# A two-layer hybrid trunk: DeltaNet's triangular inversion in 32x32 blocks, and gate and up weights in rows and places of 16 KB

## The chip, the cores and the metric

One core of a Trainium2 chip. The metric is the device time of one execution in microseconds, the median of three runs. The engines are TensorE (PE for its matmuls, PEld for its weight loads), VectorE (DVE), ScalarE (ACT), GpSimd (POOL) and SyncE (SP), which here issues every transfer from HBM.

## The reference, cut to what matters

Two layers, each a token mixer and then a mixture of experts, both closed by a layer norm. 256 tokens of width 1024, everything in float32. For the change two places matter:

```python
# gated DeltaNet, one of three mixers: 4 chunks of 64 tokens x 4 heads = 16 systems of 64x64
amat = beta[..., :, None] * jnp.einsum('bhcid,bhcjd->bhcij', k, k) * decay   # strictly lower
lhs = amat + jnp.eye(CHUNK, dtype=f32)
sol = lax.linalg.triangular_solve(lhs, rhs, left_side=True, lower=True, unit_diagonal=True)
...
# experts: 32 of them, weights 1024x512, 1024x512 and 512x1024 each, all read in every layer
for e in range(N_EXPERTS):
    h = jax.nn.silu(xt @ w_gate[e]) * (xt @ w_up[e])
    y = y + combine[:, e:e + 1] * (h @ w_down[e])
```

The expert weights of a layer are 192 MiB, those of the mixer about 50 MiB.

## The kernel before

Each layer has two stages. In the **mixer** stage the main line of work is a list of 26 blocks (`ORDER`): projections of x, branch projections and the output projection. A block's weights come in four slabs of 512 KB; each slab is split by ACT and DVE into a high and a low half (`split`, lines 252 and 264), and TensorE multiplies three times (`mm3`). The mixers' own chains (`delta_chain`, `ret_chain`, `ssd_chain`) are generators; `Weave` runs one step of each after every piece of the main line, so their matmuls stand between those of the projections. The order on each engine is fixed when the kernel is built, by the framework's scheduler, which estimates when each instruction can start; each engine, and SP's list of transfers, then runs in that order.

`delta_chain` inverts its sixteen unit lower triangular matrices by doubling. Two matrices (the two heads of a pair) stand one above the other in 128 partitions, eight such pairs side by side: a tile of 128x512. `at` is the transpose of `am` (one matmul by the identity for each block, tile `pat`). `Tn` and `Tt` hold the inverse of the diagonal blocks of size s and its transpose. In round s = 2, 4, 8, 16, 32 a mask on POOL (`mask`) cuts the blocks below the diagonal out of `at`; `px` = bt, Tn; `xx` is its copy; `pn` and `pT` are the corrections of `Tn` and `Tt` (`pn` not in the last round). Each of these products, `bmm`, is 16 matmuls of 64x64x64, on two 64x64 tiles of the array in turn: the upper pair's on rows and columns 0 to 63, the lower pair's on 64 to 127. The trace shows each float32 matmul as two weight loads and two matmul records.

In the **expert** stage eight sets of four experts follow each other. `set_front` gathers each expert's tokens with a one-hot matrix (tile `pxg`), `set_mlp` multiplies by the gate (`pg`) and up (`pu`) weights, `set_tail` by the down weights (`pdn`), `set_scatter` adds to the tokens (`acc`). The four experts of a set take 32 columns of the array each. A set's weights are 24 transfers of 1 MiB, each of 128 rows of 8 KB (`rows`, `W`): gate in two halves of four experts, up in two halves, down in two halves. Which token feature stands in which partition follows from that layout (`ROW`). The last set's down weights come in smaller pieces.

The weights live in **places** of 8 KB per partition. `ring` hands them out in a cycle: `wp` has 9; `wb` adds 6 when the mixers' working pool `mx` (20 tiles) closes after block mA; `wd` adds 2 after block mC1; `wc` adds 7 at the end of the mixer stage, 24 in all. `AT` says where in the cycle the new ones are put. A transfer waits until every reader of the place's former content is done; a mixer block takes two places, and the gain and bias of a layer norm (`W_ln`) one place each. Eight semaphores are used for the transfers, in turn, so at most eight are under way.

Of the kernel before, what the change touches and what calls it, by code (L numbers as in the profile page):

```python
# [10 lines left out]
F32 = mybir.dt.float32  # L11
# [25 lines left out]
EQ = 4  # L37
# [22 lines left out]
def _constants():  # L60

    f = np.float32
    p = np.arange(128)
    i64 = np.arange(64)
    par, loc = p // 64, p % 64
    c = {}
    c["ident"] = np.eye(128)
    c["alpha"] = np.eye(128) * ALPHA
    c["ut"] = (par[:, None] == par[None]) & (p[:, None] <= p[None])
    c["bo"] = par[:, None] == par[None]  # L70
    c["he"] = (par == 0)[:, None]
# [3 lines left out]
    for s in (1, 2, 4, 8, 16, 32):  # L75

        c[f"mt{s}"] = ((loc[:, None] // (2 * s) == i64[None] // (2 * s))
                       & (loc[:, None] % (2 * s) < s) & (i64[None] % (2 * s) >= s))
    c["m1"] = ((loc[:, None] // 2 == i64[None] // 2) & (loc[:, None] % 2 == 1) & (i64[None] % 2 == 0))
# [82 lines left out]
def trunk_kernel(ctx: ExitStack, tc: tile.TileContext, x_in, w_in, w_br, w_g, w_u, w_d, smalls, lnp, consts, out,  # L162
# [37 lines left out]


    places = ["wp"] * WP

    def ring(name="w"):
        cnt[0] += 1
        k = places.pop(0)
        places.append(k)
        return (wp if k == "wp" else pools[k][1]).tile([128, 2048], F32, name=f"{name}{cnt[0]}", tag="w")

    def more_places(name, n, side, at):  # L210
        open_pool(name, n, side)
# [3 lines left out]
        close_pool(name)  # L215
        places[:] = [k for k in places if k != name]

    def rows(src, u):

        return src[u:u + 2].rearrange("u p f -> (u p f)").rearrange("(q f) -> q f", f=2048)  # L220

    def ROW(k):

        u, j, kk = k // 4, k // 2 % 2, k % 2
        return lambda a: [a.rearrange("p (u h k q j) -> p u h k q j", h=2, k=2, q=64, j=2)[:, u, h, kk, :, j] for h in range(2)]

    def W(src):
        w = ring()
        nc.sync.dma_start(w, src)
        return w  # L230

# [171 lines left out]
    for l in range(layers):  # L403
# [254 lines left out]
        def delta_chain():  # L658
# [66 lines left out]
            pt = P("pat")  # L725
# [6 lines left out]
            DVE.tensor_copy(at, pt)  # L732
            Tn, Tt = T("Tn"), T("Tt")
            mb = lambda k: C[k][:, None, :].to_broadcast([128, 8, 64])
            POOL.tensor_mul(o8(Tn), o8(am), mb("m1"))
            POOL.tensor_sub(o8(Tn), C["e64b"], o8(Tn))
            DVE.tensor_mul(o8(Tt), o8(at), mb("mt1"))
            DVE.tensor_sub(o8(Tt), C["e64b"], o8(Tt))

            def mask(s):  # L740
                b = T("bt", True)
                POOL.tensor_mul(o8(b), o8(at), mb(f"mt{s}"))
                return b

            bt = mask(2)
# [7 lines left out]
                vb.append(vt)  # L753
            R["av"] = None
            yield
            blocks = [(n, par) for n in range(8) for par in range(2)]

            def bmm(p, a, b):
                for n, par in blocks:
                    ps, cs = slice(64 * par, 64 * par + 64), slice(n * 64, n * 64 + 64)  # L760
                    mm(p[ps, cs], a[ps, cs], b[ps, cs])

            for s in (2, 4, 8, 16, 32):
                px = P("px")
                bmm(px, bt, Tn)
                yield
                xx = T("xx", True)
                DVE.tensor_copy(xx, px)
                if s < 32:
                    bt = mask(2 * s)  # L770
                yield
                if s < 32:
                    pn = P("pn")
# [7 lines left out]
                if s < 32:  # L781
                    yield
            v4 = lambda t: t.rearrange("p (h d) -> p h d", h=4)
            yield
            for tt in range(NT):
# [527 lines left out]


        def set_front(i):
            e = EQ * i
            oh = T("oh")
            ohv = oh.rearrange("p (u t e s) -> p u t e s", u=2, t=2, e=EQ)
            it = C["iota"][:, None, None, 0:PL].to_broadcast([128, 2, EQ, PL])
            DVE.tensor_tensor(ohv[:, 0], it, bc(pv[:, :, e:e + EQ, None], PL), op=OP.is_equal)  # L1320
            POOL.tensor_mul(ohv[:, 1], ohv[:, 0], bc(cv[:, :, e:e + EQ, None], PL))  # L1321

            def gather(k0, n, copy, pin=False):

                p, t = P("pxg"), T("xg")
                for k in range(n):
                    for tt in range(NT):
                        for hh, xc in enumerate(ROW(k0 + k)(x[:, tt])):
                            m = mm(p[64 * hh:64 * hh + 64, k * 128:(k + 1) * 128], xc,
                                   oh[:, tt * 128:(tt + 1) * 128], tt == 0, tt == 1)  # L1330
# [12 lines left out]

            return gather, back

        def set_mlp(i, xg, more=None):
            e = EQ * i
            pg, pu = P("pg"), P("pu")
            for p, src in ((pg, w_g), (pu, w_u)):
                for k in range(KD):  # L1350
                    if k == len(xg):
                        xg += more(k)
                    if k % 4 == 0:
                        ws = [W(rows(src[l, e + a], k // 2)).rearrange("p (k f) -> p k f", k=4) for a in range(EQ)]
# [12 lines left out]
            return hr  # L1367
# [41 lines left out]
        def overflow(mxi):  # L1409
# [5 lines left out]
            with tc.If(rv > thresh):  # L1415
                with tc.For_i(0, NE, 1) as ei:

                    room = [wp.tile([128, 2048], F32, name=f"wo{cnt[0]}_{j}", tag="w") for j in range(WP)]
# [145 lines left out]
```

## Time and profile before

| | us |
|---|---|
| median of three runs | 1631.17 (1630.39 to 1631.46) |
| profiled execution, its own time | 1631.13 |
| its span, first to last instruction | 1629.5 |

Of the span TensorE is busy 84%, its weight loads 54%, VectorE 39%, ScalarE 31%, GpSimd 12%. The shares hide two different stages, each run through twice: mixers with a busy TensorE and a DMA that is a third busy, and experts with a DMA that is full. The page therefore has to be read in the stretches of its second part (40 slices of 40.7 us), not in its totals.

### The profile page before, as it was taken

What the parts mean: (1) busy time and instruction counts of PE and PEld (TensorE: products, weight loads), DVE (VectorE), ACT (ScalarE), POOL (GpSimd) and SP (SyncE); (2) the same over time, 40 slices, a digit from 0 to 9 for tenths busy, and PEclk for the clock granted to TensorE, in tenths of its full rate; (3) what the DMA queues carried; (4) which work ended last, traced back from release to release, by engine and by line L of the source; (5) the groups of instructions that cost most, each with busy time, mean ns of one, the idle gap of its engine ahead of it and who ended that gap; (6) DMA issues with size and microseconds to landing.
All of it is one profiled execution on the core that took longest, in us unless ns stands there. A gap on an engine that the chain in (4) does not pass through costs nothing.

```text
span 1629.5 us, 25989 instructions
## 1 busy us (share of the span) xinstructions
PE 1371.3 (84%) x10670; PEld 877.0 (54%) x10670; DVE 634.8 (39%) x1194; ACT 504.1 (31%) x997; POOL 188.2 (12%) x158
## 2 busy tenths in 40 slices
PE   8999999999877728866799999999998677287775
PEld 8999878985312203211289998799843122132211
DVE  6887777763000000000188887776620000000002
ACT  5846657541000000000067565685310000000000
POOL 0230243200000000000014212422000000000000
PEclk9999999999989959989899999999999999699889
DMA  9543333879999999999984443348799999999996
GB/s 382 182 155 130 129 131 105 317 292 411 427 427 426 427 426 426 426 427 426 409 318 132 144 141 104 134 141 346 293 408 427 428 425 426 427 427 426 427 427 257
DMA packets 90411, 518.96 MB, mean 318 GB/s; under 512 B 10032, under 2 KB 10672, under 8 KB 42928
## 3 DMA queue, kind: packets, MB, share of 16 engines
q1 hardware_dynamic: 90288, 517.25, 78.9%
q8 instruction: 86, 1.41, 0.3%
q14 instruction: 37, 0.30, 0.1%
HBM read 516.16 MB, written 1.05 MB: 317 GB/s over the span
## 4 chain that ended last, share of the span: by engine, by line
DMA 49%; PE 46%; DVE 3%; issue 1%; ACT 1%; SPq 0%; DVEq 0%
DMA w<-in_w_u_dram 19%; DMA w<-in_w_g_dram 14%; DMA w<-in_w_d_dram 14%; PE g L261 9%; PE pbr L261 6%; PE cx L261 3%; PE cz L261 3%; PE pout L261 3%; PE aq L261 1%; PE cbc L261 1%; PE av L261 1%; PE bq L261 1%; PE ak L261 1%; PE az L261 1%; PE bg L261 1%; PE pdn L261 1%
## 5 line engine op out<-in xcount | busy, mean ns | idle before, releaser
L252 DVE TENSOR_TENSOR hi<-w,hi 128x512 fp32r<-128x512 f32 x400 | 324.5, 828 | 84.2 <-ACT hi L264 37.4
L1366 DVE TENSOR_TENSOR hr<-h,pu 128x256 f32<-128x256 f32 x32 | 16.7, 599 | 726.7 <-PE pu L261 726.7
L264 ACT ACTIVATE hi<-w 128x512 fp32r<-128x512 f32 x400 | 242.8, 629 | 144.1 <-PE pbr L261 35.8
L261 PE MATMUL pg<-w,xg 128*32 128x512 f32 x1024 | 190.4, 667 | 114.4 <-DMA w<-in_w_g_dram 114.2
L261 PE MATMUL pu<-w,xg 128*32 128x512 f32 x1024 | 194.1, 673 | 61.1 <-DMA w<-in_w_u_dram 61.1
L261 PEld LDWEIGHTS pg<-w,xg 128*32 128x32 f32 x1024 | 43.7, 119 | 245.7 <-issue 138.2
L261 PE MATMUL pdn<-w,ht 128*32 128x512 f32 x1024 | 145.6, 614 | 26.5 <-DMA w<-in_w_d_dram 13.7
L261 PEld LDWEIGHTS pu<-w,xg 128*32 128x32 f32 x1024 | 45.6, 120 | 190.1 <-DMA w<-in_w_u_dram 110.0
L261 PE MATMUL g<-xh,hi 128*128 128x256 f32 x768 | 143.4, 285 | 0.0
L261 PEld LDWEIGHTS g<-xh,hi 128*128 128x128 f32 x768 | 120.7, 191 | 6.2 <-issue 5.8
L264 ACT ACTIVATE h<-pg 128x512 f32<-128x512 f32 x16 | 9.6, 597 | 338.7 <-PE pg L261 338.7
L261 PE MATMUL g<-xl,hi 128*128 128x256 f32 x384 | 108.9, 284 | 0.0
L261 PEld LDWEIGHTS pdn<-w,ht 128*32 128x32 f32 x1024 | 36.4, 112 | 121.8 <-issue 71.7
L1321 POOL TENSOR_TENSOR oh<-oh,cmb 128x256 f32<-128x256 f32 x16 | 10.0, 623 | 760.2 <-DVE oh L1320 654.9
L261 PE MATMUL pbr<-yh,hi 128*128 128x256 f32 x512 | 95.4, 283 | 0.0
L264 ACT ACTIVATE xg<-pxg 128x512 f32<-128x512 f32 (+1 forms) x18 | 10.3, 574 | 247.5 <-PE pxg L261 247.5
L264 ACT ACTIVATE os<-pdn 128x512 f32<-128x512 f32 x32 | 19.1, 596 | 215.7 <-PE pdn L261 140.9
L261 PEld LDWEIGHTS pbr<-yh,hi 128*128 128x128 f32 x512 | 80.4, 190 | 0.8 <-issue 0.3
L261 PE MATMUL pxg<-oh,x 128*64 128x128 f32 x1024 | 59.9, 274 | 21.9 <-DVE oh L1320 18.3
L261 PEld LDWEIGHTS pxg<-oh,x 128*64 128x64 f32 x1024 | 56.0, 138 | 34.9 <-issue 26.2
L261 PEld LDWEIGHTS g<-xl,hi 128*128 128x128 f32 x384 | 73.5, 191 | 0.1
L261 PE MATMUL pbr<-yl,hi 128*128 128x256 f32 x256 | 73.0, 285 | 0.0
(351 smaller groups left out, 2209.2 us busy)
## 6 DMA issues: line engine op xcount, KB each, us to landing
w<-in_w_g_dram SPq DMA_DIRECT2D x128, 1024.0 KB, 19.5
w<-in_w_u_dram SPq DMA_DIRECT2D x128, 1024.0 KB, 19.6
w<-in_w_d_dram SPq DMA_DIRECT2D x112, 1024.0 KB, 19.6
w<-in_w_in_dram SPq DMA_DIRECT2D x152, 512.0 KB, 4.7
w<-in_w_br_dram SPq DMA_DIRECT2D x48, 512.0 KB, 4.7
w<-in_w_d_dram SPq DMA_DIRECT2D x24, 512.0 KB, 11.8
ln<-in_lnp_dram SPq DMA_DIRECT2D x8, 512.0 KB, 10.7
w<-in_w_d_dram SPq DMA_DIRECT2D x16, 256.0 KB, 7.5
```

What stands on the lines that cost most here:

```text
L252: return DVE.tensor_sub(l, src, lo(h))
L261: return PE.matmul(o, l, r, start=start, stop=stop)
L264: return ACT.activation(o, i, f, **k)
L1321: POOL.tensor_mul(ohv[:, 1], ohv[:, 0], bc(cv[:, :, e:e + EQ, None], PL))
L1366: DVE.tensor_mul(hr.rearrange("p (j k h q) -> p h k q j", j=2, k=2, h=2)[:, hh], v(h), v(pu))
```

## The change

The inversion works in blocks of 32x32. The sixteen 64x64 matrices have 32 diagonal blocks; each of the four groups of 32 partitions holds eight of them side by side, 128x256 in all, and `bmm` is 32 matmuls of 32x32x32, on the four diagonal 32x32 tiles of the array in turn. The rounds are s = 2, 4, 8, 16. `Tn` and `Tt` are the halves of one tile, and both corrections come into one PSUM tile and are taken off by one DVE instruction. The block below the diagonal is done at the end: its transpose is fetched early (`pao`, 16 matmuls from partition groups 1 and 3 to 0 and 2), and two products of 16 matmuls each and their copies then fill the full 64x64 inverse (`Tf`).

The second part gives the places 16 KB: `unit` hands out a whole one, `ring` a half. `wp`, `wb`, `wd`, `wc` have 4, 3, 1 and 4 (in halves 8, 6, 2 and 8, where there were 9, 6, 2 and 7), and `mx` has 24 tiles. In all sets but the first, gate and up weights come as one transfer of 2 MiB for each expert, 128 rows of 16 KB, and `set_front` gathers in four column groups of 32 where there were two of 64. Down weights keep rows of 8 KB.

```diff
-WP, WB, WC = 9, 6, 7
-SP, MX, MS, MB, WD = 8, 20, 6, 4, 2
-AT = 4, 6, 7
+WP, WB, WC = 4, 3, 4
+SP, MX, MS, MB, WD = 8, 24, 6, 4, 1
+AT = 2, 3, 4
...
+    halves = []
+    def unit(name="w"):
+        assert not halves
         cnt[0] += 1
         k = places.pop(0)
         places.append(k)
-        return (wp if k == "wp" else pools[k][1]).tile([128, 2048], F32, name=f"{name}{cnt[0]}", tag="w")
+        return (wp if k == "wp" else pools[k][1]).tile([128, 4096], F32, name=f"{name}{cnt[0]}", tag="w")
+    def ring(name="w"):
+        if not halves:
+            w = unit(name)
+            halves.extend((w[:, 0:2048], w[:, 2048:4096]))
+        return halves.pop(0)
...
+            quarter = [slice(32 * q, 32 * q + 32) for q in range(4)]
...
+            def bmm(p, a, b):
+                for n in range(8):
+                    for q in quarter:
+                        mm(p[q, d32(n)], a[q, d32(n)], b[q, d32(n)])
+            pt, pf = P("pat"), P("pao")
             for n in range(8):
-                for par in range(2):
-                    ps = slice(64 * par, 64 * par + 64)
-                    mm(pt[ps, n * 64:n * 64 + 64], am[ps, n * 64:n * 64 + 64], ident[ps, ps])
+                for i, q in enumerate(quarter):
+                    mm(pt[q, d32(n)], am[q, c32(n, i % 2)], ident[q, q])
+            for n in range(8):
+                for e in range(2):
+                    mm(pf[quarter[2 * e], d32(n)], am[quarter[2 * e + 1], c32(n)],
+                       ident[quarter[2 * e + 1], quarter[2 * e + 1]])
...
+            for i, q in enumerate(quarter):
+                POOL.tensor_mul(o32(Tn)[q], o8(am)[q, :, 32 * (i % 2):32 * (i % 2) + 32], mb("m1")[q])
...
-            for s in (2, 4, 8, 16, 32):
+            for s in (2, 4, 8, 16):
                 px = P("px")
                 bmm(px, bt, Tn)
                 yield
-                xx = T("xx", True)
-                DVE.tensor_copy(xx, px)
-                if s < 32:
+                xx = T("xx", True)[:, :256]
+                DVE.tensor_copy(xx, px[:, :256])
+                if s < 16:
                     bt = mask(2 * s)
                 yield
-                if s < 32:
-                    pn = P("pn")
-                    bmm(pn, Tt, xx)
-                pT = P("pT")
-                bmm(pT, xx, Tt)
+                pn = P("pn")
+                bmm(pn, Tt, xx)
+                bmm(pn[:, 256:], xx, Tt)
                 yield
-                if s < 32:
-                    DVE.tensor_sub(Tn, Tn, pn)
-                DVE.tensor_sub(Tt, Tt, pT)
+                DVE.tensor_sub(TT, TT, pn)
+                yield
+            px = P("px")
+            for n in range(8):
+                for e in range(2):
+                    mm(px[quarter[2 * e + 1], d32(n)], at[quarter[2 * e], 256 + n * 32:288 + n * 32], Tn[quarter[2 * e], d32(n)])
...
+            pT = P("pT")
+            for n in range(8):
+                for e in range(2):
+                    mm(pT[quarter[2 * e], d32(n)], xx[quarter[2 * e + 1], d32(n)], Tt[quarter[2 * e + 1], d32(n)])
+            yield
+            for e in range(2):
+                act(o8(Tf)[quarter[2 * e], :, 32:64], o32(pT[quarter[2 * e], :256]), AF.Copy, scale=-1.0)
...
-                    if k % 4 == 0:
+                    if i == 0 and k % 4 == 0:
                         ws = [W(rows(src[l, e + a], k // 2)).rearrange("p (k f) -> p k f", k=4) for a in range(EQ)]
+                    elif k == 0:
+                        ws = [W2(rows(src[l, e + a], 0, 4)).rearrange("p (k f) -> p k f", k=8) for a in range(EQ)]
                     for a in range(EQ):
                         ps = slice(PL * a, PL * a + PL)
-                        mm(p[ps], xg[k][:, ps], ws[a][:, k % 4], k == 0, k == KD - 1)
+                        mm(p[ps], xg[k][:, ps], ws[a][:, k % (4 if i == 0 else 8)], k == 0, k == KD - 1)
```

## Rows read from the trace of the kernel before

**Rows 1.** The page's second part: busy tenths of 40 slices, and GB/s.

```profile
PE   8999999999877728866799999999998677287775
DMA  9543333879999999999984443348799999999996
GB/s 382 182 155 130 129 131 105 317 292 411 427 427 426 427 426 426 426 427 426 409 318 132 144 141 104 134 141 346 293 408 427 428 425 426 427 427 426 427 427 257
```

**Rows 2.** Stretches: length, busy us of five engines (instructions), granted clock, DMA share, GB/s.

```profile
20.00:30.00 10.00, 10.00 (x86) 10.00 (x85) 9.64 (x27) 7.69 (x14) 0.00 (x0) 1.00 1.02 419
...
100.00:160.00 60.00, 60.00 (x743) 56.29 (x743) 47.23 (x104) 35.32 (x59) 5.03 (x6) 1.00 0.42 139
...
342.50:362.50 20.00, 20.00 (x91) 16.50 (x90) 13.86 (x22) 6.29 (x12) 1.29 (x1) 1.00 0.59 193
362.50:385.00 22.50, 20.86 (x145) 13.10 (x145) 13.74 (x56) 2.88 (x8) 0.67 (x1) 1.00 1.00 414
385.00:387.50 2.50, 2.50 (x40) 1.89 (x44) 0.00 (x0) 0.60 (x1) 0.00 (x0) 1.00 0.73 218
387.50:700.00 312.50, 228.81 (x1626) 79.44 (x1618) 16.32 (x32) 17.64 (x32) 3.70 (x6) 0.90 1.01 426
```

**Rows 3.** The chain that ended last, 88 to 172 us: start, us, what.

```profile
88.57 1.15 PE pat L261 x32
...
96.21 1.08 PE px L261 x32
97.29 3.30 PE cx L261 x26
100.59 1.08 PE pn L261 x32
101.67 0.93 PE pT L261 x32
...
167.04 0.49 PE pT L261 x12
...
167.97 0.73 PE pT L261 x20
```

**Rows 4.** Instructions in order of time: four column tiles of 32, 512 columns each.

```profile
516.41 3.63 PE L261 MATMUL pg<-w,xg 128*32 128x512 f32 x28 [1.03 <-DMA w<-in_w_g_dram]
```

**Rows 5.** SP's transfers around the end of the first mixer stage.

```profile
331.45 0.80 SPq L229 DMA_DIRECT2D w<-in_w_g_dram  x2
334.99 19.19 SPq L229 DMA_DIRECT2D w<-in_w_d_dram  x5
360.60 0.33 SPq L229 DMA_DIRECT2D w<-in_w_g_dram  x1
363.51 2.98 SPq L229 DMA_DIRECT2D w<-in_w_u_dram  x6
368.12 2.29 SPq L229 DMA_DIRECT2D w<-in_w_d_dram  x2
...
384.95 5.80 SPq L229 DMA_DIRECT2D w<-in_w_g_dram  x5
```

**Rows 6.** What SP waited for from 280 to 420 us: total, times, longest.

```profile
SPq L229 <- DVE hi L252: 43.6, 10, 6.5
SPq L229 <- PE pg L261: 12.4, 2, 11.4
```

**Rows 7.** Instructions in order of time: the last set's tail, first and second layer.

```profile
786.23 6.52 PE L261 MATMUL pu<-w,xg 128*32 128x512 f32 x26 [1.40 <-DMA w<-in_w_u_dram]
...
1593.65 3.62 PE L261 MATMUL pu<-w,xg 128*32 128x512 f32 x26 [1.46 <-DMA w<-in_w_u_dram]
...
1599.97 3.41 PE L261 MATMUL pdn<-w,ht 128*32 128x512 f32 x22 [0.78 <-DVE ht L1385]
...
1611.88 3.63 PE L261 MATMUL pdn<-w,ht 128*32 128x512 f32 x28 [2.24 <-DMA w<-in_w_d_dram]
```

**Rows 8.** The page's third part: a DMA queue's packets, MB, share of 16 engines.

```profile
q8 instruction: 86, 1.41, 0.3%
```

More of the change, by code (lines that the diff above doesn't have):

```diff
@@ L74, in _constants @@
     c["madd"] = np.where(i64[None] < loc[:, None], 0.0, -30000.0)
[L75 to L79, printed above, removed]
+    i32, l32 = np.arange(32), p % 32
+    for s in (1, 2, 4, 8, 16):
+        c[f"mt{s}"] = ((l32[:, None] // (2 * s) == i32[None] // (2 * s))
+                       & (l32[:, None] % (2 * s) < s) & (i32[None] % (2 * s) >= s))
+    c["m1"] = (l32[:, None] // 2 == i32[None] // 2) & (l32[:, None] % 2 == 1) & (i32[None] % 2 == 0)
+    c["d32"] = l32[:, None] == i32[None]
     inv = (f(10000.0) ** (-np.arange(0, 128, 2, dtype=f) / f(128))).astype(f)
@@ L216, in fewer_places, with rows, ROW, W2 @@
         places[:] = [k for k in places if k != name]
[L218 to L225, printed above, removed]
+    def rows(src, u, n=2):
+        return src[u:u + n].rearrange("u p f -> (u p f)").rearrange("(q f) -> q f", f=1024 * n)
+    def ROW(k, n):
+        u, j, kk = k // (2 * n), k // 2 % n, k % 2
+        return lambda a: [a.rearrange("p (u h k q j) -> p u h k q j", h=n, k=2, q=128 // n, j=n)[:, u, h, kk, :, j]
+                          for h in range(n)]
     def W(src):
         w = ring()
+        nc.sync.dma_start(w, src)
+        return w
+    def W2(src):
+        w = unit()
         nc.sync.dma_start(w, src)
@@ L724, in delta_chain @@
             yield
-            pt = P("pat")
-            for n in range(8):
-                for par in range(2):
-                    ps = slice(64 * par, 64 * par + 64)
-                    mm(pt[ps, n * 64:n * 64 + 64], am[ps, n * 64:n * 64 + 64], ident[ps, ps])
+            quarter = [slice(32 * q, 32 * q + 32) for q in range(4)]
+            c32 = lambda n, r=0: slice(n * 64 + 32 * r, n * 64 + 32 * r + 32)
+            d32 = lambda n: slice(n * 32, n * 32 + 32)
+            o32 = lambda a: a.rearrange("p (n j) -> p n j", j=32)
@@ L730, in delta_chain @@
             yield
             at = T("at")
[L732 to L738, printed above, removed]
+            DVE.tensor_copy(at[:, :256], pt[:, :256])
+            for e, eng in ((0, DVE.tensor_copy), (1, act)):
+                eng(at[quarter[2 * e], 256:], pf[quarter[2 * e], :256])
@@ L740, in mask @@
+            TT = T("Tn")
+            Tn, Tt = TT[:, :256], TT[:, 256:]
+            mb = lambda k: C[k][:, None, :].to_broadcast([128, 8, 32])
+            for i, q in enumerate(quarter):
+                POOL.tensor_mul(o32(Tn)[q], o8(am)[q, :, 32 * (i % 2):32 * (i % 2) + 32], mb("m1")[q])
+            POOL.tensor_sub(o32(Tn), mb("d32"), o32(Tn))
+            DVE.tensor_mul(o32(Tt), o32(at[:, :256]), mb("mt1"))
+            DVE.tensor_sub(o32(Tt), mb("d32"), o32(Tt))
             def mask(s):
-                b = T("bt", True)
@@ L742, in mask @@
-                POOL.tensor_mul(o8(b), o8(at), mb(f"mt{s}"))
+                b = T("bt", True)[:, :256]
+                POOL.tensor_mul(o32(b), o32(at[:, :256]), mb(f"mt{s}"))
                 return b
@@ L755, in delta_chain @@
             yield
[L756 to L761, printed above, removed]
-            for s in (2, 4, 8, 16, 32):
+            for s in (2, 4, 8, 16):
                 px = P("px")
@@ L766, in delta_chain @@
                 yield
-                xx = T("xx", True)
-                DVE.tensor_copy(xx, px)
-                if s < 32:
+                xx = T("xx", True)[:, :256]
+                DVE.tensor_copy(xx, px[:, :256])
+                if s < 16:
                     bt = mask(2 * s)
                 yield
-                if s < 32:
-                    pn = P("pn")
-                    bmm(pn, Tt, xx)
-                pT = P("pT")
-                bmm(pT, xx, Tt)
-                yield
-                if s < 32:
-                    DVE.tensor_sub(Tn, Tn, pn)
-                DVE.tensor_sub(Tt, Tt, pT)
-                if s < 32:
-                    yield
+                pn = P("pn")
+                bmm(pn, Tt, xx)
+                bmm(pn[:, 256:], xx, Tt)
+                yield
+                DVE.tensor_sub(TT, TT, pn)
[4 more added lines that the diff above has]
+                    mm(px[quarter[2 * e + 1], d32(n)], at[quarter[2 * e], 256 + n * 32:288 + n * 32], Tn[quarter[2 * e], d32(n)])
+            Tf = T("Tt")
+            POOL.tensor_copy(o8(Tf)[:, :, 0:32], C["zero"][:, :, None].to_broadcast([128, 8, 32]))
+            for i, q in enumerate(quarter):
+                (POOL.tensor_copy if i < 2 else act)(o8(Tf)[q, :, 32 * (i % 2):32 * (i % 2) + 32], o32(Tt)[q])
+            yield
+            xx = T("xx", True)
+            for e, eng in ((0, DVE.tensor_copy), (1, act)):
+                eng(xx[quarter[2 * e + 1], :256], px[quarter[2 * e + 1], :256])
+            yield
+            pT = P("pT")
+            for n in range(8):
+                for e in range(2):
+                    mm(pT[quarter[2 * e], d32(n)], xx[quarter[2 * e + 1], d32(n)], Tt[quarter[2 * e + 1], d32(n)])
+            yield
+            for e in range(2):
+                act(o8(Tf)[quarter[2 * e], :, 32:64], o32(pT[quarter[2 * e], :256]), AF.Copy, scale=-1.0)
+            Tt = Tf
             v4 = lambda t: t.rearrange("p (h d) -> p h d", h=4)
@@ L1315, in set_front @@
         def set_front(i):
-            e = EQ * i
+            e, nr = EQ * i, 2 if i == 0 else 4
             oh = T("oh")
@@ L1416, in overflow @@
                 with tc.For_i(0, NE, 1) as ei:
-                    room = [wp.tile([128, 2048], F32, name=f"wo{cnt[0]}_{j}", tag="w") for j in range(WP)]
+                    room = [wp.tile([128, 4096], F32, name=f"wo{cnt[0]}_{j}", tag="w") for j in range(WP)]
+                    room = [r[:, c:c + 2048] for r in room for c in (0, 2048)]
                     ws = []
```

5 lines of the change are left out of this document (2 added, 3 removed).

## The prediction

> **What bounds the kernel now.** I read the slices first [rows 1]: four stages, two with PE at 9 tenths and DMA at 3 to 5 (mixers), two with DMA at 9 (experts). The stretches [rows 2] say how hard each limit is. From 100 to 160 us PE is busy 60.00 of 60.00 us at full clock while DVE has 47 and DMA 0.42 of its time: the mixer is TensorE's. From 387.5 to 700 us DMA has a share of 1.01 and 426 GB/s while PE has 229 of 312 us: the expert stage is the DMA's, and PE's clock (0.90) matters there only at its end. The chain [rows 3] confirms the first: it runs through PE alone, and the inversion's products stand on it one after the other between projections. Between the stages lies a third stretch that belongs to neither: from 342.5 to 362.5 us DMA has only 0.59 [rows 2], because SP waits for places, 43.6 us on weights not yet split [rows 6]. From 362.5 on DMA is full but for one hole, 385 to 387.5 us (0.73), where SP waits for set 0's gate to free a place [rows 5, 6]. So whatever still has to be loaded when the last places open, at 360.6 us [rows 5], shifts the end one to one. That is the view that decides here.
>
> **Part 1, the inversion on PE.** Before, for each layer: pat 1.15 us, five px at 1.08, four pn at 1.08, four pT at 0.93 and the last in two pieces, 0.49 and 0.73 [rows 3] (one row of each kind stands, the chain of the first layer has the others): 1.15 + 5.40 + 4.32 + 3.72 + 1.22 = 15.8 us, all on the chain. A product that follows its own kind takes 0.93 us for 32 records, 29 ns each; coming from another shape it costs 0.15 more (1.08). Two tiles are in turn, so each tile steps every 58 ns; 64 columns passed twice at 2.4 GHz are 53, so about 5 ns are fixed.
>
> After: 32 (pat) + 16 (pao) + 4 rounds of 96 + 16 + 16 = 464 matmuls, 928 records where there were 480. No row has tiles of 32x32. By the same step, 32 columns passed twice are 27 ns, with 5 fixed 32 ns; with four tiles in turn a record takes 8 ns, with two (pao and the two last products) 16. 832 x 8 + 96 x 16 = 8.2 us, and 11 changes of shape at 0.15 make 9.8. **Saved: 6.0 us a layer.** Ends: if the four tiles gave nothing over today's two, 29 ns a record, it would be 928 x 29 + 1.65 = 28.6 us, a loss of 12.8; if records cost half my 8 and 16, 5.8 us, a gain of 10. I take 8 ns, by the one row in which four tiles are in turn: 28 records of 512 columns in 3.63 us [rows 4], 0.11 us apart where one alone needs 2 x 512 / 2.4 = 0.43, so four do overlap. The changes of shape are as many as before, and the chain has as many steps in the weave, 20, so what follows stands at the same piece of the main line.
>
> The rest of this part costs nothing: DVE's copies and subtractions halve in width, POOL gets more but smaller instructions, ACT five short ones; they hide under the projections that stand between the steps (3.30 us of cx between px and pn [rows 3]). If that cover were gone, a late copy would stop PE for its own length, under 1 us.
>
> The Trainium skill, "TensorEngine Tiling (Array Packing)", Gotcha 1, speaks against this: different row tiles cannot access the same PSUM bank simultaneously. All four tiles of a product write one bank here, so by it they would take turns, 32 ns a record. By that rule, the trace disagrees: today's two row tiles write one bank too, and their records follow each other every 29 ns where one tile alone steps every 58 [rows 3].
>
> **Part 2, rows of 16 KB.** In the mixer's beginning DMA is full with rows of 4 KB at 419 GB/s, in the expert stage with rows of 8 KB at 426 [rows 2]. A sixteenth of that gives 156.4 ns for 4 KB and 307.7 for 8, so 5.1 ns are fixed and 16 KB take 610.3, 429.5 GB/s. Seven sets have 112 MiB of gate and up, 448 such rows on each of the 16 engines: 448 x 5.1 = **2.3 us a layer saved**. Ends: the second doubling gains as much as the first in rate (433 GB/s, 4.5 us), or as much is lost. That packets of 16 KB exist is seen in the instruction queue: 86 of them are 1.41 MB [rows 8].
>
> **Part 3, places of 16 KB.** A place now comes free only when both its halves are read. Inside the mixer this hides: a block takes one whole place, comes free three blocks ahead, and DMA has more than half its time left [rows 2]. Before the experts it does not. I walked the cycle of places through both programs. Before, the places that open at 360.6 us and later are wc's seven (one w_g, six w_u [rows 5]) and the two that hold the layer norm's gain and bias (two w_d at 368.12): 9 MiB. At 426 GB/s a MiB is 2.46 us, so 22.1 us, to 382.7; the full stretch ends at 385, and the hole follows. After, wc has eight halves, and the cycle falls so that block o1's first half shares its place with the gain, the bias shares the next with o1's second half: 4 MiB of set 0's down weights wait for the layer norm where two did. 12 MiB, 29.5 us, to 390.1. What comes before 360.6 has slack (0.59) and SP's order stays by availability. So 3 MiB more, 7.4 us, less the hole that is then filled (0.27 x 2.5, and its start: 1.2 us) and about 1 us because the first opened place now holds 2 MiB and bridges the gap from 360.60 to 363.51. **Lost: 5.0 us a layer**; ends 0 (the scheduler issues so that slack takes it) and 7.4. In the slices layer 2 has the same pattern [rows 1].
>
> Within the sets nothing waits more: a place's next transfer comes a set later (58 us), and eight transfers under way are now up to 16 MiB, so SP runs further ahead, not less.
>
> **Part 4, the tail.** The four experts' matmuls can start in earnest only when the fourth's whole 2 MiB has landed: 58 records stand behind the last landing of up where 26 do [rows 7]. At full clock 26 take 3.62 us, at half 6.52, so 32 more are 3.9 to 7.3 us. Down weights, 8 MiB, need 19.7 us more to land, and PE waits for them until 1611.88 us though it began pdn at 1599.97 with 3.41 us of work: that cover hides the added records at full clock, not all of them at half. **Lost: 0.5 us a layer**, ends 0 and 4.5. The wider gather (64 matmuls a set in four column groups, not 32 in two) has PE's idle quarter in the expert stage as cover.
>
> **The sum**: -6.0 - 2.3 + 5.0 + 0.5 = -2.8 a layer, -5.6 for both. Against the profiled execution's own 1631.13 us (1.6 above its span, 0.04 below the median): **1625.5 us**.
>
> **Rivals.** *Two tiles in turn are all that overlaps* (slower): then each record takes 32 / 2 = 16 ns, 928 x 16 + 1.65 = 16.5 us, 0.7 more than before in place of 6.0 less; 1625.5 + 2 x 6.7 = 1639. It decides from 11.8 ns a record, where the inversion's gain falls to 3.2 and the sum to zero. For it: the closest records in the rows stand 29 ns apart. Against: rows 4. If nothing overlapped, 32 ns, 31.3 us: 1669; against that stand rows 3. *The late places cost nothing*: the down weights of set 0 are the last it needs, and if the added 3 MiB find slack, 10 us fall away: 1615.5. Against: from 387.5 us on there is no hole in which to make them up. *The rows do not do what they say*: cut into pieces of 8 KB, or no faster: 1625.5 + 4.6 = 1630. For it: two rates of whole GB/s carry the whole term.
>
> **How the numbers follow.** Forecast 0.50, with a range of its own of 1618 to 1632 from Parts 3 and 4; two tiles in turn 0.17, nothing overlapped 0.05; late places free 0.16; rows without effect 0.12. The range goes from 1614 to 1640: it leaves out the 0.05, and half of what lies about the edges. A measurement of this kernel can tell 0.2%, 3.3 us, from no change. Faster than that (under 1627.9): 0.42 of the forecast's 0.50, the 0.16, 0.02 of the rows': 0.60. Within it: 0.08 and 0.10: 0.18. Slower: 0.22.
>
> **What would show it.** Right: records of px and pn 8 ns apart, the inversion's pieces on the chain about 10 us a layer, the mixer's end 6 us earlier; w_g and w_u at 429 to 430 GB/s in sets 1 to 7; DMA full from the last places' opening past set 0 with no hole, 12 MiB issued from there and not 9; pdn of the last set still ending on a DMA wait. Wrong: records at 16 ns or more; a slice of PE idle in the mixer because a copy or a place comes late; a share under 1 between sets.

## The result, and the profile after

The changed kernel takes 1643.91 us (median of four runs, 1643.19 to 1648.25) beside 1630.78 for the kernel before (four runs): a ratio of 1.0085, 95% interval 1.0073 to 1.0097, 13 us slower. The forecast was 1625.5, its range ended at 1640. The profiled execution has a span of 1641.5 us (before 1629.5).

The page of the changed kernel: four rows of the 40 slices, then the instruction queue (packets, MB, share).

```profile
PE   8999999999757718754899999999997676186646
PEclk9999999999978859877999999999998789598768
DMA  9344234869999999999954342338699999999995
GB/s 386 143 157 155 104 125 144 323 275 430 428 427 431 427 430 429 427 429 431 405 216 140 120 155 103 148 140 325 277 429 429 428 430 428 429 427 428 430 429 231
...
q8 instruction: 100, 1.64, 0.4%
```

Beside [rows 1] the stages and their limits are the same: PE in the mixers, DMA in the experts, and the experts' rate is some 2 GB/s higher; the instruction queue has 14 packets more [rows 8]. PE's row is unchanged in the mixers and lower in the experts (7 and 5 tenths for 8 and 7), and its clock falls there. Nothing in this view explains 13 us. So the stretches, with the columns of [rows 2]:

```profile
100.00:160.00 60.00, 59.89 (x964) 56.38 (x963) 48.66 (x101) 40.44 (x68) 9.98 (x12) 1.00 0.37 134
...
361.00:390.00 29.00, 27.36 (x231) 14.61 (x233) 11.26 (x50) 5.19 (x11) 0.67 (x1) 1.00 1.02 429
...
387.50:700.00 312.50, 206.63 (x1934) 75.86 (x1926) 16.32 (x32) 16.36 (x31) 3.70 (x6) 0.84 1.01 429
```

In the mixer PE is still full at full clock, with some 220 instructions more than before in the 60 us. From 361 us on DMA is full with no hole; before there was one at 385 [rows 2]. In the experts DMA moves 429 GB/s for 426, and PE's granted clock has fallen to a mean of 0.84 from 0.90.

The inversion itself on the chain (start, us, what), answering [rows 3]:

```profile
81.74 0.72 PE pat L279 x48
82.46 0.51 PE pao L279 x32
...
89.88 0.68 PE px L279 x50
90.56 3.06 PE cx L279 x24
93.63 1.22 PE pn L279 x82
...
159.91 0.30 PE pT L279 x10
...
160.65 0.49 PE pT L279 x22
```

A round's first product takes 0.68 us where it took 1.08, and one pn of 1.22 stands for what were a pn and a pT (1.08 and 0.93). With four rounds of px and pn (one pn there takes 1.5), the first layer's inversion is 10.5 us on the chain in place of 15.8.

SP's transfers at the end of the first mixer, answering [rows 5], and ahead of the last set of layer 2:

```profile
330.54 12.04 SPq L242 DMA_DIRECT2D w<-in_w_d_dram  x4
356.16 5.88 SPq L242 DMA_DIRECT2D w<-in_w_u_dram  x8
363.67 4.96 SPq L242 DMA_DIRECT2D w<-in_w_d_dram  x4
...
1544.72 0.33 SPq L247 DMA_DIRECT2D w<-in_w_g_dram  x1
1547.14 5.29 SPq L247 DMA_DIRECT2D w<-in_w_u_dram  x3
...
1559.40 7.68 SPq L247 DMA_DIRECT2D w<-in_w_g_dram  x3
1571.58 0.33 SPq L247 DMA_DIRECT2D w<-in_w_u_dram  x1
```

Eight of up and four of down, of 1 MiB each, are issued from the last places' opening on: 12 MiB where 9 were. No part of the prediction has the other four lines: the scheduler puts three of the last set's up weights ahead of three of its gate weights. What that does to the tail stands in PE's instructions in order of time (start, us, line, operation, tiles, count, and the idle time before), answering [rows 7]:

```profile
1598.41 9.22 PE L279 MATMUL pg<-w,xg 128*32 128x512 f32 x58 [2.93 <-DMA w<-in_w_g_dram]
...
1607.50 7.43 PE L279 MATMUL pu<-w,xg 128*32 128x512 f32 x56
1617.62 4.49 PE L279 MATMUL pdn<-w,ht 128*32 128x512 f32 x36 [0.78 <-DVE ht L1434]
...
1623.95 3.63 PE L279 MATMUL pdn<-w,ht 128*32 128x512 f32 x28
```

Behind the last landing of gate stand 58 records of gate and then 56 of up, 16.5 us of PE without a break, and pdn no longer waits for a down weight: the end belongs to PE, where before it was the DMA's.

How far single milestones moved against the kernel before (us, last matmul of each group in the two traces; minus is earlier). "Inversion" is the end of bg, which lies behind most of its products, "mixer" the end of pout, "experts" that of acc. The kernels of the experiments are in the same table.

| kernel | start, aq | inversion | mixer | experts | layer 2: aq | inversion | mixer | experts |
|---|---|---|---|---|---|---|---|---|
| changed | -2.4 | -8.2 | -4.5 | +1.1 | +1.7 | +2.4 | +6.3 | +12.1 |
| e1, inversion alone | -0.8 | -6.1 | -2.3 | -2.6 | -2.6 | -7.0 | -2.0 | -0.4 |
| e2, places and rows alone | -2.0 | -2.0 | -2.1 | +5.0 | +5.6 | +5.5 | +5.6 | +13.6 |
| e3, layer norm's own place | -1.4 | -7.1 | -3.4 | -2.7 | -2.1 | -3.9 | +0.9 | +1.0 |
| e11, half a packet shifted | -2.7 | -8.7 | -4.9 | +0.9 | +1.6 | -2.6 | +2.2 | +7.9 |
| e8, inversion and fewer table loads | -1.7 | -7.9 | -7.3 | -7.4 | -7.4 | -11.4 | -10.8 | -9.1 |

The first row shows three kinds of loss: between "inversion" and "mixer" in both layers (3.7 and 3.9 us), in the experts of both (5.6 and 5.8), and in layer 2's inversion, which gains nothing (+1.7 to +2.4). The start differs by up to 2.7 us between these programs before any product of the change has run; the cause is open. Each trace is one execution: e1's took 2.1 us more than the median of its runs, e2's 2.9 more, e3's 3.6 less, the others lie within 1.6.

The experts' loss splits at the last landing of a down weight in the traces. "Load" is the time from the mixer's end to that landing, "tail" the time from there to the end of acc (us):

| kernel | layer 1: load | tail | layer 2: load | tail |
|---|---|---|---|---|
| before | 441.9 | 4.4 | 441.6 | 3.9 |
| changed | 447.3 | 4.5 | 444.4 | 7.0 |
| e4, order of the last set kept | 447.4 | 4.6 | 444.3 | 4.3 |
| e3, layer norm's own place | 442.5 | 4.5 | 439.6 | 6.0 |
| e6, last set in 8 KB rows and order kept | 442.9 | 6.1 | 440.3 | 3.8 |
| e10, all sets in 8 KB rows and order kept | 444.8 | 4.9 | 442.0 | 3.8 |

So layer 2's 5.8 us are 2.8 of load and 3.1 of tail, layer 1's are load alone. A tail moves by itself as well: in e1 and e8, whose last set is that of the kernel before, layer 2's is 5.5, since the last 28 records of pdn take 5.32 us there and 3.63 in the kernel before. In every kernel with the larger places layer 1's load is 2.5 to 3.2 us longer than layer 2's, before it was 0.3. One more transfer stands in it there: constants of the next layer (`mc`, 1187.5 KB), issued at 793.8 us and landed at 802.6 among the last down weights; the kernel before issues it at 821.0, behind the stage. At 429 GB/s it takes 2.8 us.

### The profile page after: what moved, and what is told of

Same layout as the page of the kernel before. It is cut to its first block, busy times and chain, and to the rows that moved or that the text cites. A ratio compares the mean times of both kernels' runs of the same rounds, so it can differ in the third digit from the quotient of the medians.

```text
span 1641.5 us, 29244 instructions
## 1 busy us (share of the span) xinstructions
PE 1315.0 (80%) x12462; PEld 870.5 (53%) x12462; DVE 622.4 (38%) x1186; ACT 511.1 (31%) x1011; POOL 186.0 (11%) x168
## 4 chain that ended last, share of the span: by engine, by line
PE 48%; DMA 46%; DVE 3%; ACT 2%; issue 1%; POOL 1%; SPq 0%; DVEq 0%; ACTq 0%; POOLq 0%
DMA w<-in_w_d_dram 17%; DMA w<-in_w_g_dram 15%; DMA w<-in_w_u_dram 13%; PE g L279 7%; PE pbr L279 6%; PE cx L279 3%; PE pg L279 3%; PE pout L279 3%; PE cz L279 2%; PE pu L279 2%; PE cbc L279 1%; PE aq L279 1%; PE bq L279 1%; PE av L279 1%; PE ak L279 1%; PE bk L279 1%
## 5 line engine op out<-in xcount | busy, mean ns | idle before, releaser
L279 PE MATMUL pg<-w,xg 128*32 128x512 f32 x1024 | 185.7, 717 | 216.9 <-DMA w<-in_w_g_dram 216.9
L282 ACT ACTIVATE hi<-w 128x512 fp32r<-128x512 f32 x392 | 237.6, 628 | 122.8 <-PE pbr L279 34.1
L279 PE MATMUL pu<-w,xg 128*32 128x512 f32 x1024 | 165.4, 677 | 31.6 <-DMA w<-in_w_u_dram 31.6
L279 PE MATMUL pdn<-w,ht 128*32 128x512 f32 x1024 | 122.1, 601 | 12.7 <-DVE ht L1434 12.7
L279 PE MATMUL pxg<-oh,x 128*32 128x128 f32 (+1 forms) x1920 | 65.1, 289 | 25.2 <-DVE oh L1366 21.7
L279 PEld LDWEIGHTS pxg<-oh,x 128*32 128x32 f32 (+1 forms) x1920 | 61.2, 141 | 37.8 <-issue 28.1
```

Of the source, the lines that this page charges most:

```text
L279: return PE.matmul(o, l, r, start=start, stop=stop)
L282: return ACT.activation(o, i, f, **k)
```

## The experiments

Medians, with the kernel before run beside each on the same chip:

| run | median us | before | ratio, 95% interval |
|---|---|---|---|
| e1_inv | 1629.07 | 1631.17 | 0.9987 (0.9978 to 0.9995) |
| e2_oldinv | 1641.79 | 1631.17 | 1.0061 (1.0048 to 1.0074) |
| e3_ln | 1636.45 | 1631.17 | 1.0041 (1.0028 to 1.0054) |
| e4_order | 1641.68 | 1631.17 | 1.0071 (1.0059 to 1.0083) |
| e5_rows8 | 1632.18 | 1631.39 | 1.0007 (0.9998 to 1.0016) |
| e6_last8 | 1627.67 | 1631.39 | 0.9984 (0.9975 to 0.9993) |
| e7_pad | 1648.54 | 1631.39 | 1.0110 (1.0096 to 1.0125) |
| e8_pre2 | 1622.82 | 1631.39 | 0.9954 (0.9941 to 0.9967) |
| e9_best | 1620.25 | 1631.57 | 0.9939 (0.9927 to 0.9952) |
| e10_rows8pin | 1631.18 | 1631.57 | 1.0006 (0.9994 to 1.0019) |
| e11_pad32 | 1640.54 | 1631.57 | 1.0071 (1.0056 to 1.0087) |
| e12_act | 1631.37 | 1631.57 | 1.0003 (0.9994 to 1.0012) |

An interval is about 2 us wide to each side, so a difference of two medians below carries up to 3 us.

**The two halves apart.** e1 puts the new constants and the new inversion into the kernel before, e2 puts the old ones into the changed kernel.

> The kernel before with the inversion in 32x32 blocks alone; places, rows and the order of the transfers stay as they were. The step on record says -6.0 us a layer, 1630.8 - 12 = 1619. The trace of the changed kernel says otherwise: there az began 9.0 us earlier in layer 1, but 4.5 us of it were given back between az and the output projection, where crm and xdt of the state-space chain stand on the chain of waits, and in layer 2 nothing was gained. Theory A (the give-back belongs to the inversion: what stood under its long products comes late when they are short): -2 to -4 us in all, 1627 to 1629, and the same waits on crm and xdt. Theory B (the give-back belongs to the larger places, whose weights come later): close to 1619, no such waits.

> The changed kernel with the old inversion in 64x64 blocks: places of 16 KB and rows of 16 KB alone; SP's order of transfers is that of the changed kernel. Theory A (the two halves add up, and the inversion is worth -2 to -4 us): 1646 to 1648, slower than the changed kernel. Theory B (the inversion gains its 12 us where places leave it alone, and the places spoil it): about 1644, like the changed kernel. In both the last down weights of layer 1 land about 5 us later after the opening of the last places than before, and in layer 2 the matmuls of the tail end some 4 us further behind the last transfer than before.

Alone the inversion is worth 2.1 us, not 12; places and rows alone cost 10.6. Theory A for e1: the table shows 5.3 us gained in layer 1 up to bg (-0.8 to -6.1) and 3.8 of them lost again before pout, in layer 2 4.4 and 5.0, with the old places. e2 came out below both numbers, 2.1 us under the changed kernel, which is within the noise: there the inversion shows no worth. In e1's chain PE is absent between az, a projection, and py, a product of the state-space chain that reads crm:

```profile
222.25 1.28 ACT L266
...
225.77 1.28 ACT L266
...
227.81 1.28 ACT L266
...
230.26 1.59 DVE hi L254
...
232.24 4.00 DMA w<-in_w_in_dram
236.24 0.63 ACT crm L266
...
236.94 1.28 POOL crm L1035
...
238.27 1.15 PE py L263 x32
```

Three of four table loads of ACT, instructions that bring in the functions it is to evaluate (the fourth is at 223.86), then its split of a weight, DVE's half of the split, and crm, for which py waits. The chain puts a transfer between the split and crm, but that transfer held nothing up: crm reads no weight, and ACT's part of it begins at 236.23, before the landing, right behind a fifth table load. What stands there is in the lists of DVE and ACT; the last line is crm's end in the kernel before.

```profile
233.56 0.69 DVE L1032 TENSOR_TENSOR crm<-gcl,pcr 128x512 f32<-128x512 f32 x1
...
234.94 1.28 ACT L266 ACT_TABLE_LOAD   x1
236.23 0.63 ACT L266 ACTIVATE crm<-crm 128x512 f32<-128x512 f32 x1
...
235.29 1.30 POOL L1005 TENSOR_TENSOR crm<-crm,cb 128x512 f32<-128x512 f32 x1 [0.69 <-ACT crm L264]
```

DVE takes up crm at 233.56, behind two halves of splits for which it waited on ACT. In the kernel before, crm ends at 236.59 us and py begins at 238.70: 2.1 us to spare. With the new inversion PE has done what stands ahead of py 2.4 us earlier than before, at 236.26, and crm ends at 238.21, 1.6 us later than before, because the scheduler now puts az's SiLUs between cf's logarithm and exponential, four table loads where there were three. So PE stands still for 2.0 us and begins py only 0.4 us earlier than before; ahead of poT it stands still for another 0.9. The changed kernel has the same two stops, 2.0 and 0.9 to 1.0 us, in both layers.

**Fewer table loads.** e8 is e1 with one table loaded that serves both the logarithm and the exponential, and az's SiLUs put behind them; e12 has the same edit on the kernel before.

```
+            ln_exp_after(mark["sq"])
+            mark["cf"] = rstd_small(cf, cf, 1.0 / 128)
...
+            ln_exp_after(mark["sc"])
             rstd_small(rs, ssc, 1.0 / 512)
...
+                if n == "az":
+                    with tc.issue_after(mark["cf"].ins):
+                        act(t, p, f)
```

> The inversion alone in 32x32 blocks on the kernel before, with fewer table loads on ACT: one table that has both logarithm and exponential is loaded ahead of cf and ahead of crs, and az's two SiLUs come behind cf's exponential and not in between; four table loads become two at cf, one goes at crs. What is computed stays the same. With the inversion alone the chain of waits runs there through ACT: loads at 222.25, 223.86, 225.77 and 227.81 us, then hi on ACT, hi on DVE, a place, a transfer of 4.0 us, crm, and PE stands still 2.2 us ahead of py; 1.1 us more behind the loads of crs; in layer 2 about 3.9 and 0.5. Theory A (ACT's chain with its loads gives the inversion's gain back): 2.6 and 1.3 us less on that chain, of the 7.7 us given back 4 to 6 return: 1623 to 1625. Rival (the give-back is set by the weights' places or by POOL): 1628 to 1629.

> The kernel before, with its old inversion, its places and rows, and the fewer table loads on ACT alone. Theory A (before, ACT's chain ended just in time under PE's work, and only the shorter inversion uncovers it): no change, 1630 to 1631.5, and PE without a stop from az to the output projection. Rival (the loads cost time in the kernel before too): 1625 to 1627.

1622.82: 6.3 us less than e1, a little more than the 4 to 6 expected. e8's chain in the same stretch:

```profile
226.48 8.85 PE cz L263 x39
235.33 1.08 PE py L263 x32
...
273.42 1.75 PE poT L893 x16
```

PE alone, and py 2.9 us earlier than in e1; crm now ends at 233.64, 1.7 us ahead of py. On the kernel before the same edit moves nothing (1631.37 beside 1631.57), though its trace has a stop of 1.0 us ahead of poT in either layer, where theory A had none. Both fit: the table loads cost nothing as long as the old inversion covers them, and most of the new inversion's gain once it doesn't. Fewer loads and the later SiLUs came in one edit; no run tells them apart. The Trainium skill, "ScalarE: Activation LUTs", section "Table sets: the hidden batching unit", says that a logarithm and an exponential behind it take one load, from a set that holds both; in e1's trace there are loads ahead of each of the two, and one only where that set is asked for, as in e8.

**The layer norm's place.** e3 gives gain and bias one place of 16 KB, so that o1's halves share another.

```
-        r = []
+        r, w = [], whole("ln")
...
-            r.append(ring("ln")[:, 0:1024])
+            r.append(w[:, 1024 * j:1024 * j + 1024])
```

> The changed kernel, but the first layer norm's gain and bias get a place of 16 KB of their own, and block o1's two halves share one, so that one place and not two waits for the layer norm. 10 MiB in place of 12 are issued from the opening of the last places on. Theory A (what is still to load at that point shifts the end one to one): 2 MiB at 429 GB/s are 4.9 us a layer less, 1643.9 - 9.8 = 1634. Rival (the added load finds slack, the loss is elsewhere): 1642 to 1644.

7.5 us less; 9.8 were expected. SP's transfers in e3:

```profile
331.65 19.66 SPq L246 DMA_DIRECT2D w<-in_w_d_dram  x6
357.26 5.91 SPq L246 DMA_DIRECT2D w<-in_w_u_dram  x8
366.74 0.81 SPq L246 DMA_DIRECT2D w<-in_w_d_dram  x2
```

Two down weights went ahead of the opening, 10 MiB are left. From "mixer" to "experts" layer 1 loses 0.7 us in place of 5.6, layer 2 0.1 in place of 5.8. The load is 4.8 us shorter in either layer, beside 4.9 worked out for 2 MiB; the rest in layer 2 is tail. So what is still to load there moves the last landing one to one.

**The last set.** e4 keeps the order of the last set's transfers, gate before up; e6 is e3 with that order and with 8 KB rows in the last set; e5 is e3 with 8 KB rows in all sets and the scheduler's order; e10 is e6 with 8 KB rows in all sets.

```
-                    if i == 0 and k % 4 == 0:
+                    if (i in (0, NB - 1)) and k % 4 == 0:
```

> The changed kernel with the gate and up weights of the last set of each layer kept in the order in which the program has them: gate's four, then up's four. In the changed kernel the scheduler put three of up ahead of three of gate, so the gate's products start late and 56 of the up products stand behind them. Theory A (that order costs the 4 us by which layer 2's end stands further behind the last transfer): 1643.9 - 4 = 1640, with up's last products at most 30 records behind up's last landing. Rival (the larger transfers themselves make the tail late, since four experts' 2 MiB land nearly together): 1643 to 1644 and a tail as long as in the changed kernel.

> The kernel with the layer norm's own place, the last set of each layer in rows of 8 KB, and its transfers kept in the program's order, gate before up; sets 1 to 6 keep rows of 16 KB. In the kernel with the layer norm's place PE works without a break from gate's last landing (1588.3 us) to the last down product (1616.5). Theory A (landings of whole experts and up ahead of gate make layer 2's tail TensorE's): the tail goes back to a wait on the last down weights, 1 to 3 us less in layer 2, nothing in layer 1, where constants of the next layer lie between the down weights: 1634 to 1635. Rival (the tail is the same length whatever lands first, since the down weights end it): 1636 to 1637.

> The kernel with the layer norm's own place, but with gate and up of every set in rows of 8 KB, two transfers into each place of 16 KB: it tells what the 16 KB rows are worth by themselves. Theory A (Part 2 on record: 2.3 us a layer): 4.6 us more than the kernel with the layer norm's place, less 1 to 2 us that its tail gets back because an expert's first half lands by itself: 1639 to 1640. Rival (the rows are worth nothing, the larger landings cost the tail): 1634 to 1636.

> The kernel with the layer norm's own place, 8 KB rows and gate before up in the last set, but with rows of 8 KB in sets 1 to 6 as well: against the one with 16 KB rows there (1627.7) it tells what the 16 KB rows are worth without the tail. Theory A (Part 2 on record, six of its seven sets): 2.0 us a layer, 1631.6. Rival (8 KB rows cost nothing): 1627 to 1628.

Order alone is worth 2.2 us with 16 KB rows (e4; 4 were expected) and 1.0 with 8 KB rows (e5 to e10), both within the noise of the medians; in the traces e4's tail is 2.7 us shorter than the changed kernel's in layer 2 and as long in layer 1. In e4 58 records still stand behind up's last landing, 9.00 us; the "at most 30" was wrong, since the matmuls go through k before they change the expert, so that nearly all of them wait for the last expert's row. Order and 8 KB rows together give 8.8 in the medians (e3 to e6), far more than 1 to 3. The traces don't bear that out as tail: it is 2.2 us shorter in layer 2 and 1.6 longer in layer 1, and the two executions differ by 3.7 us in all, most of it the stops told of next (3.0 in e3's trace, none in e6's). What else made e3's other executions slower is not shown. e6's tail:

```profile
1582.49 3.63 PE L285 MATMUL pu<-w,xg 128*32 128x512 f32 x28 [1.36 <-DMA w<-in_w_u_dram]
...
1592.31 3.62 PE L285 MATMUL pu<-w,xg 128*32 128x512 f32 x26 [1.37 <-DMA w<-in_w_u_dram]
...
1609.88 3.62 PE L285 MATMUL pdn<-w,ht 128*32 128x512 f32 x26 [0.17 <-DMA w<-in_w_d_dram]
```

Up comes in two halves of 28 and 26 records, each taken at full clock, and pdn waits for the DMA again, as in [rows 7]. e6 and e10 differ in sets 1 to 6 alone: 16 KB rows are worth 3.5 us there (1627.67 and 1631.18), where 4.0 were worked out; the loads differ by 2.0 and 1.7. e5's expectation missed by 7 us, 3.0 of them because e3, its base, carries the stops told of next, and e5 doesn't; the rest is not shown.

**PE's stops in layer 2.** The chain of the changed kernel in layer 2's inversion:

```profile
911.53 0.63 PE px L279 x47
912.16 2.24 issue
914.41 0.33 PE px L279 x6
...
950.57 1.18 PE pn L279 x80
951.75 1.52 issue
953.27 0.25 PE pn L279 x3
```

PE stands still within a product, for nothing that the profile names. A packet of 16 KB of the instruction queue begins at 912.09 us and another at 950.88; eight more begin between 896 and 955 us without such a stop. e7 adds 64 matmuls between the layers, e11 32.

```
+                for _ in range(32 if warm and tt == 0 else 0):
+                    tc.keep_in_program_order(mm(p[0:32, 0:32], ident[0:32, 0:32], cst[0:32, 0:32]))
```

> The changed kernel with 64 small matmuls more (32x32, on data that is there) on PE while it waits for the layer norm between the layers; nothing else differs, and their 2 us lie in PE's wait. In the changed kernel PE stands still in layer 2's inversion 2.24 and 1.52 us inside a product, for nothing that the profile shows, each time while a packet of 16 KB of the instruction queue is under way; in three programs these stops stand behind the same matmuls of the program, number 7329 and 8095, 766 apart, six packets' worth. Theory A (PE waits for its own instructions, at fixed places of its stream): the stops stay at matmul 7329 and 8095 of the stream, now 64 matmuls earlier in the inversion, or vanish where the instructions in front are slow ones; they don't stay behind the same matmul of the product px. Rival (a wait on data or on another engine that the profile doesn't name): they stay behind the same matmul of the inversion, now 7393 and 8159. Time between 1640 and 1645.

> The changed kernel with 32 small matmuls more between the layers. The 64 of the run before were 128 records, 128 pairs of a weight load and a matmul, exactly one packet of instructions, so that run could not move the stops against the program. 32 are 64 records, half a packet. In ten programs every stop of over 0.6 us in layer 2's inversion lies at record 31 to 34 of a period of 128, whatever product stands there. Theory A (PE waits for its instructions at the border of a packet): the stops of 2.24 and 1.52 us in px and pn go away; one of 0.6 to 1.4 us may stand at record 33 of a period in the projections; layer 2's inversion gains 2 to 3 us, and the time is 1641 to 1642. Rival (data): the stops stay in px and pn behind the same matmuls, 1644.

e7 could not tell: 64 matmuls are 128 records, a whole period, and the stops stayed in px and pn (1.30 and 1.33 us), as either theory has it; it also came out slower than expected (1648.54); in its trace, of an execution of 1642.54 us, the added matmuls delay layer 2 by 1.4 us, and the rest is not explained. e11 tells. The stop in px is gone, that in pn too, and one is left in the projections:

```profile
909.01 1.43 PE cx L279 x12
910.44 0.94 issue
911.38 0.87 PE cx L279 x6
912.25 0.68 PE px L279 x50
...
947.36 1.22 PE pn L279 x82
948.58 3.06 PE cbc L279 x24
```

It stands behind record 7329 of the program, as the one in px did before the shift: the stop belongs to a place in PE's stream, not to a product. 3.4 us less in the medians, little more than their noise; in the traces layer 2's inversion is 4.9 us shorter, 2.8 of them in these stops. e11's text says ten programs; it is the eight with the new inversion run until then, whose stops of over 0.6 us in this stretch all lie at 31 to 34 of 128 records, in px or pn where PE takes a record every 8 to 10 ns, and otherwise in cx, where the starts of two records are 0.6 to 1.4 us apart and PE stands still for 0.3 to 1.1. The two kernels with the old inversion have one of 0.7 us elsewhere, ahead of a product, where the profile names DVE's copy. A record is a weight load and a matmul, so 128 are 256 instructions. The Trainium skill, "Runtime: NRT & Kernel Launch", section "Instruction fetch mechanics", says that each engine's instructions come in blocks of 16 KiB, 256 instructions, and that crossing a border is mostly hidden; the trace agrees with the first by its period, and with the second only in the projections. In e1 the border falls into cx, since its program has 448 records fewer ahead, three periods and a half. Layer 1's inversion has one stop of that kind, in a pn, at record 90 of 128: 0.66 us in e1, 0.3 to 0.4 in three more, none in the others. Why it is smaller there, and why most borders pass without one, is open.

**All together.** e9 is e6 with e8's edit.

> All that helped at once: the 32x32 inversion, places of 16 KB with a place of its own for the layer norm, 16 KB rows in sets 1 to 6, 8 KB rows and gate before up in the last set, and the fewer table loads on ACT. Theory A (the parts add up; ACT's loads were worth 6.3 us on the inversion alone): 1627.7 - 6.3 = 1621.4, 1620 to 1623. Rival (the places make the mixer wait for weights where ACT no longer does): 1625 to 1628.

1620.25 us, as expected: 0.6% faster than the kernel before (0.9927 to 0.9952), 24 us faster than the changed kernel; PE is busy for 85.00 of the 85 us from 200 to 285.

## Why the prediction was wrong

**Part 1** was right in what the inversion costs (9.8 us worked out, 10.5 on the chain) and in its reason: four tiles overlap. The Trainium skill, "TensorEngine Tiling (Array Packing)", section "Gotcha 1: PSUM Pressure", says that different row tiles cannot access one PSUM bank simultaneously. By that rule, with the tiles in turn, it would have been 31 us; the trace disagrees, since 128 records of a pn, in four row tiles and one bank, take 1.22 us. The failed step is the sentence that the rest of this part "costs nothing". I took a full PE for proof that PE alone sets the mixer's end. It says that what PE waits for was ready so far, not by how much. The chain through ACT had 2.1 us to spare at py, too little for 6 us of saved PE time. The price that Part 1 put on a late copy, under 1 us, was too low as well: PE stands still for 2.0 us ahead of py and 0.9 ahead of poT. Of 12 us for both layers 2.1 arrived (e1); e8 and e12 show that ACT's table loads and the place of the SiLUs held back 6.3 more, so that 8.6 of the 12 come with e8.

A second cost was not in the sum: PE's own instructions. The change puts 928 records where 480 stood, in bursts, and I priced them by their columns and a fixed part alone; the queue of instructions was in [rows 8], read only for its packet size. The stops are 3.8 us in the trace, all in layer 2, and e11 gives 3.4 back in the medians, by the luck of where a border falls. That they are a wait for instructions is inferred from their place and period; the profile names no cause.

**Part 2** held: 1.75 us a layer for six sets in the medians of e6 and e10, 2.0 and 1.7 in the loads of their traces, 2.0 by its step. The rival that rows change nothing is out.

**Part 3** held in mechanism and size: 12 MiB, and 2 of the 3 MiB taken back shorten the load by 4.8 us in either layer's trace, where 4.9 were worked out; the medians give 7.5 for both. It had no term for `mc`, which the scheduler moved among layer 1's down weights (2.8 us).

**Part 4** failed, by its order and not by its price. It put 0.5 us a layer, on the step that gate and up land in the program's order and that down weights' 19.7 us cover the added records. Where that order is kept (e4), the tail is 0.1 and 0.4 us longer than before, with 58 records behind up's last landing. With the new places the scheduler orders them otherwise, and the records that stand behind a landing came twice, 58 of gate and 56 of up, the first in part at the lower clock (9.22 us, granted clock 0.66 on average from 1560 to 1600 us, a mix of the levels of 1.2 and 2.4 GHz, with PE busy for 16 of these 40 us). Layer 2's tail grew by 3.1 us (1.5 beside the 5.5 of e1 and e8), layer 1's by 0.1, where `mc` holds up the last down weights too. Both are within the ends of 0 and 4.5 that I had written and then left out of my value. The order itself was in no row; I could have read that the scheduler puts transfers by availability, as I said in Part 3, and not have relied on it in Part 4.

The sum in the two traces, which lie 12.1 us apart at the last acc where the forecast had 5.6 less (us, layer 1 and 2): mixers -2.1 and +4.6, where Part 1 had -6.0 each; loads +5.4 and +2.8, where Parts 2 and 3 had +2.7 each; tails +0.1 and +3.1, where Part 4 had 0.5 each; ahead of the first inversion and between the layers -2.4 and +0.6, where there was no term. So of the 17.7 us missed 14.5 are Part 1's, 2.8 the loads', as much as `mc` takes, and 2.2 the tail's. The medians give no second check of this: from e1 by e10, e6 and e3 to the changed kernel they step by -2.1, +2.1, -3.5, +8.8 and +7.5, which add up to the 12.8 between the kernels by construction, and each step carries up to 3 us. None of the rivals came true. Tiles did overlap, the late places were not free, rows worked. I had no rival in which the gain of Part 1 is hidden by another engine, though DVE's 47 and ACT's 35 us of busy time in 60 [rows 2] invited one.

## What to carry to other kernels

A PE that is busy all the time says nothing about the slack behind it: before a saving on the bound engine is counted, follow one dependent step (here py) back through the other engines and see how late its last releaser came. When buffers are made larger, list for each what shares it and what is issued when the last one opens; and write down the order of the last transfers, since a scheduler may not keep it. Very short instructions can cost time by their bytes too, and then a shift by a few instructions can be worth as much as an edit.

## What the runs showed of the hardware

- Products of 32x32 in four row and column tiles, all in one PSUM bank: 128 records in 1.22 us, 9.5 ns each, where two tiles of 64x64 took 29 (0.93 us for 32).
- PE's stream in layer 2's inversion has stops a multiple of 128 records apart, at some of these borders: 0.3 to 1.1 us where the instructions are projections, 1.3 to 2.2 within 32x32 products.
- Rows of 16 KB move 428 to 429 GB/s where rows of 8 KB move 426, and with them PE's mean granted clock in the expert stage is 0.85 and not 0.90 (e6 and e10, 390 to 700 us), with PE busy for 201 and not 220 of 310 us.
- ACT's table load takes 1.28 us; in e1 logarithm and exponential load one each, in e8, where a table with both is asked for, one serves the two.
